# Two sparse attention layers on one Trainium2 core: where the selection of a block's keys ranks among the attention's steps

## The chip, the cores and the metric

The kernel runs on one core of one Trainium2 chip. The metric is the device time in microseconds (us) of one execution; the smaller the better. TensorE (PE in the profile) multiplies matrices into PSUM; VectorE (DVE), ScalarE (ACT) and GpSimd (POOL) do the elementwise work; SyncE (SP) starts the weights' transfers. Each engine works off its own instructions in the order in which the built program has them, and waits where an instruction's inputs or buffers are not ready.

## The reference

The model takes 512 tokens of width 1024 through one block of a first kind and then two layers of a second kind. The change lies in the second kind's sparse attention, cut here to what matters:

```python
def dsa_attention(q, k, v, qi, ki, wi):        # T = 512, 8 heads of 64; topk = 128; blocks of 128 queries
    def block_fn(args):
        rel = jax.nn.relu(jnp.einsum('bqhd,bsd->bqhs', qib, ki32))      # 4 index heads
        score = jnp.einsum('bqh,bqhs->bqs', wib, rel)
        score = jnp.where(visible[None], score, -jnp.inf)               # key_pos <= qpos
        _, idx = lax.top_k(score, topk)
        k_sel, v_sel = gather(k, idx), gather(v, idx)
        logits = jnp.einsum('bqhd,bqkhd->bhqk', qb, k_sel) * scale      # masked by idx <= qpos
        p = jax.nn.softmax(logits, axis=-1)
        return jnp.einsum('bhqk,bqkhd->bqhd', p, v_sel)
```

Beside this attention each layer runs a gated recurrence of four heads (hgrn) on the same input. Both results go through a projection, are weighted by sigmoid gates and added, and a feed-forward part follows. Queries and keys are normed by head and rotated (RoPE) before the attention.

## The kernel before

All weights are streamed from HBM in 512 KB pieces; ScalarE and GpSimd or VectorE split each piece into a high and a low part (`whi`, `wlo`, lines 149 and 152), and each product is three matmuls (lines 168 to 170 where the output has tokens on the partitions, 193 to 195 where it has features). One such matmul of 512 columns is called wide here; a projection of one 128 wide column tile is 24 of them.

A layer of the second kind (`second_mix`) first writes down the attention (`dsa`), then the four recurrence heads, each with three projections (hf, hq, hg) and a chain of small steps (lines 466 to 515), then two merges: the attention's with eight gate projections and eight output projections (`gate`, `merge`), then the recurrence's. A scheduler orders the instructions of each engine: what is written earlier ranks ahead of what is written later, weights and evictions ahead of all, and what is not ready by its reckoning lets later work pass. So the recurrence heads' projections and the first three gate projections fill the attention's waits on TensorE.

Within the attention the string `ORDER` (line 25) says in which order the steps are written down:

- `x`: the projection of the index inputs; `h`: that of the recurrence's values; `X`: rotation and transposes of the index inputs (line 863), from which come `iqT` and `ikT`.
- `1`, `2`, `3`: `select(i)`, the selection of block i's keys. For each of four index heads TensorE multiplies (line 874) into w = (i+1)*128 columns, ScalarE takes the Relu (876) and VectorE weights and adds (879, 881); after a mask (882) come 16 rounds in which `max` finds the eight largest scores of each row (885) and `match_replace` marks them as taken (886); line 887 turns the marks into a bias. Block 0 needs no selection, since it has 128 keys.
- `k`, `q`, `v`: the projections of keys, queries and values; ScalarE copies them out and squares them (810, 812), VectorE sums the squares (813). `K`: rotation of the keys (`rotated`): the square root's steps (229 to 233), two products on VectorE and two on GpSimd for each block (799 to 802), the scaling (825), and the transposes on TensorE (239).
- `Q`: the same for one block of queries at each call; its results `qT` are kept until the attention of that block.
- `a` to `d`: `attend(i)`, the attention of blocks 0 to 3. For each of eight heads: scores on TensorE (925), bias and negative maximum on VectorE (927), the exponential on ScalarE (929), transposes (933), a copy (935), and the products with the values (937) into one PSUM tile. Then the division (939, 941), transposes (239) and the split into high and low (217, 218).

All PSUM tiles of the attention's lane are drawn from two banks (`BANKS`, tag `pa`). During `attend` the output tile holds one, so that a head's scores and its transposes take turns in the other.

The loop that writes the steps down, and the rounds of the selection:

```python
        for c in ORDER:
            if c in steps:
                steps[c]()
            elif c in "123":
                select(int(c))
            else:
                attend("abcd".index(c))

            for r in range(16):
                m8 = self.small("m8", 8)
                nc.vector.max(m8, sc[:, 0:w])
                nc.vector.match_replace(sc[:, 0:w], m8, sc[:, 0:w], TAKEN)
```

Of the kernel before, what the change touches and what calls it, by code (L numbers as in the profile page):

```python
# [21 lines left out]
KD = 8  # L22
KF = 22
WARM = 12
ORDER = "xhX123kKqvQaQbQcQd"
EPS = 1e-6
NEG = -1e30
UNSEEN = -2e38
# [42 lines left out]
class Builder:  # L71
# [756 lines left out]
    def dsa(self, l, X):  # L828
# [61 lines left out]
        def inputs(j, name):  # L890
            got[name] = self.attention_inputs(A["w_tok"][l, j], X, name)
# [23 lines left out]
        def attend(i):  # L915
# [27 lines left out]
            for m in range(4):  # L943
# [3 lines left out]
                     q=lambda: inputs(1, "aq"), Q=rotate_query, v=values, h=gated_values)  # L947
        for c in ORDER:
            if c in steps:
# [155 lines left out]
```

## Time and profile before

| what | value |
|---|---|
| median of three runs | 2590.12 us (2587.59 to 2593.46) |
| the profiled execution's own time | 2592.11 us |
| its span, first to last instruction | 2590.3 us |
| mean granted clock of TensorE | 0.99 |
| attention and recurrence, first layer of the second kind | from about 876 to 1310 us of the span |
| the same, second layer | from about 1730 to 2168 us |

The span is the time from the first to the last instruction; the execution's own time has 1.8 us around it. In the sections below, "first layer" and "second layer" are these two. A matmul's busy time in the trace is longer than the spacing of two matmuls that follow each other, since they overlap; the spacing is the price of one in a full stretch. The granted clock is 1.00 at 2.4 GHz and 0.50 at 1.2 GHz.

### The profile page before, as it was taken

Reading aid. Unit: us, or ns where it says so; the run is one execution under the profiler, and the core shown is the slowest. Engines: PE = TensorE matmul, PEld = TensorE weight load, DVE = VectorE, ACT = ScalarE, POOL = GpSimd, SP = SyncE. Lnnn points to the kernel's source line nnn. Section 1 sums busy time; section 2 is a strip of 40 time slices with the busy share of each in tenths; the row PEclk is TensorE's granted clock in tenths of the full one; section 3 lists DMA queues with packets and bytes.
Section 4 is the critical chain, followed back from the end, with each engine's and each line's share of the span. In section 5 each row is a group of like instructions: output and inputs, shape, how many; then the busy total and the mean of one; then the engine's idle time right before and its main releaser. Section 6 shows DMA issues by size and latency. Waiting matters only on the chain.

```text
span 2590.3 us, 31616 instructions
## 1 busy us (share of the span) xinstructions
PE 2504.4 (97%) x11742; PEld 2047.2 (79%) x11742; DVE 1362.4 (53%) x2568; ACT 1011.7 (39%) x1830; POOL 769.8 (30%) x676
## 2 busy tenths in 40 slices
PE   9999999999999998899999999999798999999999
PEld 7877888888888766777888888887677788888887
DVE  4675222477764677765244444336877523444432
ACT  5633333444443344453343333334355333433322
POOL 4234334511101333643361110013465335211100
PEclk9999999999999999999999999999899999999999
DMA  4112233322233222111332223332211123222233
GB/s 136 58 60 82 87 97 98 102 98 98 97 95 96 76 74 73 42 37 59 94 99 98 97 94 95 94 98 66 73 42 40 34 96 101 96 94 96 97 108 88
DMA packets 67434, 217.66 MB, mean 84 GB/s; under 512 B 7744, under 2 KB 8640, under 8 KB 67280
## 3 DMA queue, kind: packets, MB, share of 16 engines
q1 hardware_dynamic: 67280, 215.65, 26.1%
q8 instruction: 92, 1.51, 0.2%
q14 instruction: 62, 0.51, 0.1%
HBM read 213.52 MB, written 2.10 MB: 83 GB/s over the span
## 4 chain that ended last, share of the span: by engine, by line
PE 80%; DVE 14%; POOL 3%; issue 2%; ACT 1%; DMA 0%; SPq 0%; DVEq 0%; POOLq 0%; ACTq 0%
PE mm L194 23%; PE mm L195 23%; PE mm L193 23%; DVE score L886 2%; DVE m L885 2%; PE at L925 1%; PE at L937 1%; PE at L239 1%; DVE wlo L152 1%; POOL hG L495 1%; PE mm L169 1%; PE mm L170 1%; PE mm L168 1%; DVE rsq_w L231 1%; PE at L933 1%
## 5 line engine op out<-in xcount | busy, mean ns | idle before, releaser
L149 ACT CAST whi<-wraw 128x512 fp32r<-128x512 f32 (+3 forms) x824 | 502.3, 610 | 1139.9 <-PE mm L195 950.4
L193 PE MATMUL mm<-xh,wlo 128*128 128x512 f32 x1920 | 759.0, 395 | 0.0
L194 PE MATMUL mm<-xl,whi 128*128 128x512 f32 x1920 | 758.2, 395 | 0.0
L195 PE MATMUL mm<-xh,whi 128*128 128x512 f32 x1920 | 755.5, 393 | 0.0
L152 DVE TENSOR_TENSOR wlo<-wraw,whi 128x512 fp32r<-128x512 f32 (+1 forms) x529 | 385.2, 728 | 458.5 <-ACT whi L149 455.4
L152 POOL TENSOR_TENSOR wlo<-wraw,whi 128x512 fp32r<-128x512 f32 (+2 forms) x295 | 381.4, 1293 | 760.5 <-ACT whi L149 689.6
L195 PEld LDWEIGHTS mm<-xh,whi 128*128 128x128 f32 x1920 | 361.8, 188 | 74.5 <-issue 1.9
L194 PEld LDWEIGHTS mm<-xl,whi 128*128 128x128 f32 x1920 | 361.9, 188 | 73.5 <-issue 1.7
L193 PEld LDWEIGHTS mm<-xh,wlo 128*128 128x128 f32 x1920 | 361.8, 188 | 72.9 <-issue 1.2
L193 PE MATMUL mm<-acth,wlo 128*128 128x512 f32 x528 | 205.4, 389 | 0.0
L194 PE MATMUL mm<-actl,whi 128*128 128x512 f32 x528 | 205.4, 389 | 0.0
L195 PE MATMUL mm<-acth,whi 128*128 128x512 f32 x528 | 205.4, 389 | 0.0
L733 POOL TENSOR_TENSOR fg<-fg,rstd 128x512 f32<-128x512 f32 x44 | 56.7, 1289 | 425.6 <-ACT fg L732 425.6
L168 PE MATMUL mm<-wlo,xh 128*128 128x512 f32 (+2 forms) x384 | 147.0, 383 | 17.3 <-POOL wlo L152 9.2
L169 PE MATMUL mm<-whi,xl 128*128 128x512 f32 (+2 forms) x384 | 145.2, 378 | 0.2 <-DVE xl L288 0.2
L170 PE MATMUL mm<-whi,xh 128*128 128x512 f32 (+2 forms) x384 | 145.1, 379 | 0.0
L202 DVE TENSOR_TENSOR gate<-mm,rstd 128x512 f32<-128x512 f32 x56 | 38.7, 691 | 165.2 <-PE mm L195 164.3
L277 POOL TENSOR_TENSOR acc<-acc,sq 128x512 f32<-128x512 f32 x39 | 58.9, 1509 | 199.2 <-ACT sq L274 198.3
L194 PEld LDWEIGHTS mm<-actl,whi 128*128 128x128 f32 x528 | 99.1, 188 | 20.8
L193 PEld LDWEIGHTS mm<-acth,wlo 128*128 128x128 f32 x528 | 99.1, 188 | 20.6
L195 PEld LDWEIGHTS mm<-acth,whi 128*128 128x128 f32 x528 | 99.1, 188 | 20.4
L168 PEld LDWEIGHTS mm<-wlo,xh 128*128 128x128 f32 x384 | 73.4, 191 | 36.1 <-POOL wlo L152 11.7
(352 smaller groups left out, 3333.1 us busy)
## 6 DMA issues: line engine op xcount, KB each, us to landing
wraw<-in_w_ffn_in SPq DMA_DIRECT2D x88, 512.0 KB, 3.3
wraw<-in_w_gate SPq DMA_DIRECT2D x56, 512.0 KB, 3.3
wraw<-in_w_in SPq DMA_DIRECT2D x52, 512.0 KB, 3.3
wraw<-in_w_up SPq DMA_DIRECT2D x44, 512.0 KB, 3.2
wraw<-in_w_tok SPq DMA_DIRECT2D x32, 512.0 KB, 3.2
wraw<-in_w_ffn_out SPq DMA_DIRECT2D x32, 512.0 KB, 3.6
wraw<-in_w_down SPq DMA_DIRECT2D x16, 512.0 KB, 3.6
wraw<-in_w_po SPq DMA_DIRECT2D x32, 256.0 KB, 2.6
```

The lines of the kernel that those rows point to most:

```text
L149: nc.scalar.copy(wh, raw[:, k:k + m, :])
L152: eng.tensor_tensor(wl, raw[:, k:k + m, :], wh.bitcast(F32), op=OP.subtract)
L168: nc.tensor.matmul(ps[t][:, 0:w], xh, wl, start=i == 0, stop=False)
L169: nc.tensor.matmul(ps[t][:, 0:w], xl, wh, start=False, stop=False)
L170: nc.tensor.matmul(ps[t][:, 0:w], xh, wh, start=False, stop=i == KD - 1)
L193: nc.tensor.matmul(ps, wl, xh, start=i == 0, stop=False)
L194: nc.tensor.matmul(ps, wh, xl, start=False, stop=False)
L195: nc.tensor.matmul(ps, wh, xh, start=False, stop=i == n - 1)
L277: (nc.vector if d % 2 and len(acc) > 1 else nc.gpsimd).tensor_tensor(a, a, sq, op=OP.add)
L733: nc.gpsimd.tensor_tensor(g, g, self.rstd, op=OP.mult)
L885: nc.vector.max(m8, sc[:, 0:w])
L886: nc.vector.match_replace(sc[:, 0:w], m8, sc[:, 0:w], TAKEN)
```

## The change

One string is changed. The selections no longer stand together ahead of the keys' projection: each stands just ahead of its block's attention. And two blocks of queries are rotated ahead of the first attention, and each later block one attention earlier.

```diff
-ORDER = "xhX123kKqvQaQbQcQd"
+ORDER = "xhXkKqvQQa1Qb2Qc3d"
```

What this does to the engines' orders is shown at three places of the first layer; the second layer's change in the same way. (A row is one instruction or several equal ones; `score` is the selection's row of scores, `m` the eight largest, `ak` and `rsq` belong to the keys' norm, `rope` and `aro` to rotation, `aon` to the division at an attention's end, `csts` holds the identity for transposes.)

**VectorE, where the keys are normed and rotated.** Before, between the rounds of the second selection:

```order
L813 TENSOR_REDUCE akss<-asq 128x8 x2
L885 MAX m_7689<-score 128x8
L820 TENSOR_SCALAR akss<-akss 128x32
L800 TENSOR_TENSOR rope_7968<-akx,tabS 128x8x32
L152 TENSOR_TENSOR wlo<-wraw,whi 128x512
L886 MATCH_REPLACE score<-m_7689,score 128x384
L229 TENSOR_SCALAR rsq_y<-akss 128x32
L801 TENSOR_TENSOR rope_7968<-akx,tabS 128x8x32
L885 MAX m_7692<-score 128x8
L231 TENSOR_TENSOR rsq_w<-akss,rsq_y 128x32
```

Now:

```order
L800 TENSOR_TENSOR rope_7755<-akx,tabS 128x8x32
L813 TENSOR_REDUCE akss<-asq 128x8 x2
L801 TENSOR_TENSOR rope_7755<-akx,tabS 128x8x32
L820 TENSOR_SCALAR akss<-akss 128x32
L229 TENSOR_SCALAR rsq_y<-akss 128x32
L231 TENSOR_TENSOR rsq_w<-akss,rsq_y 128x32
L152 TENSOR_TENSOR wlo<-wraw,whi 128x512
L232 SCALAR_TENSOR_TENSOR rsq_w<-rsq_w,rsq_y 128x32
```

The selection's rounds have gone from this place; the keys' steps follow each other with only the weights' split between them.

**TensorE, at the last block's attention (512 keys).** Before, the step from one of its heads to the next:

```order
L193 MATMUL mm<-xh,wlo 128x512
L933 MATMUL at<-csts,aL 128x128 x4
L194 MATMUL mm<-xl,whi 128x512
L195 MATMUL mm<-xh,whi 128x512
L193 MATMUL mm<-xh,wlo 128x512
L194 MATMUL mm<-xl,whi 128x512
L937 MATMUL at<-av,aPT 128x64 x4
L925 MATMUL at<-kT,qT 128x512
```

Now, from the end of the third block's attention (384 keys) into the last's:

```order
L925 MATMUL at<-kT,qT 128x384
L933 MATMUL at<-csts,aL 128x128 x3
L937 MATMUL at<-av,aPT 128x64 x3
L239 MATMUL at<-csts,aon 128x128 x4
L874 MATMUL at<-ikT,iqT 128x512 x4
L925 MATMUL at<-kT,qT 128x512
L933 MATMUL at<-csts,aL 128x128 x4
L937 MATMUL at<-av,aPT 128x64 x4
```

The wide matmuls of gate projections that stood between the steps of a head now stand ahead of the third block's attention, and the third selection's score matmuls (874) stand between the two attentions.

**VectorE, at the same place.** Before, two heads of the last block, with steps of the fourth recurrence head around them:

```order
L514 TENSOR_TENSOR hf<-hf,hq 128x512
L927 ISA aL,anm<-at,score 128x512
L927 ISA anm 128x1
L399 COPY rS<-at 128x128
L401 SCALAR_TENSOR_TENSOR rS<-rS,dec,at 128x128 x2
L411 TENSOR_REDUCE rss<-rsq 128x4
L412 TENSOR_SCALAR rss<-rss 128x4
L229 TENSOR_SCALAR rsq_y<-rss 128x4
```

Now, between the third block's last head and the last block's first:

```order
L939 RECIPROCAL aden<-aden 128x8
L941 TENSOR_TENSOR aon<-at,aden 128x512
L218 TENSOR_TENSOR yal<-at,yah 128x128 x2
L879 TENSOR_SCALAR score<-rel,iw 128x512
L218 TENSOR_TENSOR yal<-at,yah 128x128
L212 TENSOR_TENSOR yhl<-ry,yhh 128x512 x2
```

Behind these rows come the rest of the third selection's scores and its 16 rounds, and only then the last block's eight heads; the fourth recurrence head's steps now lie ahead of all this.

## Rows read from the trace of the kernel before

**Rows 1.** The page's first part: TensorE's busy time, share of the span.

```profile
PE 2504.4 (97%) x11742; PEld 2047.2 (79%) x11742; DVE 1362.4 (53%) x2568; ACT 1011.7 (39%) x1830; POOL 769.8 (30%) x676
```

**Rows 2.** Busy time by stretch; four of the first layer, one of the second.

```profile
core 0: us, PE busy (x) PEld busy (x) DVE busy (x) ACT busy (x) POOL busy (x), PEclk, DMA share, GB/s
924.00:1017.00 93.00, 81.18 (x334) 61.42 (x335) 86.48 (x207) 37.96 (x80) 34.37 (x28) 0.94 0.21 68
1017.00:1049.00 32.00, 28.90 (x157) 22.63 (x157) 19.88 (x46) 18.77 (x41) 14.62 (x17) 1.00 0.16 51
1049.00:1198.00 149.00, 136.61 (x832) 108.89 (x832) 109.81 (x253) 70.05 (x143) 74.78 (x82) 1.00 0.11 35
1198.00:1310.00 112.00, 112.00 (x500) 92.84 (x500) 33.13 (x52) 36.73 (x63) 38.92 (x30) 1.00 0.30 92
...
1901.00:2057.00 156.00, 144.25 (x834) 115.61 (x834) 110.69 (x257) 69.94 (x143) 79.27 (x85) 0.95 0.10 33
```

**Rows 3.** TensorE's waits, 876 to 1310: us, times, longest.

```profile
PE at L239 <- DVE aro L825: 13.6, 4, 8.3
...
PE at L933 <- ACT aL L929: 2.2, 1, 2.2
```

**Rows 4.** VectorE's groups by shape, 924 to 1021: busy us, mean ns, idle before.

```profile
L885 DVE MAX8 m<-score 128x8 f32<-128x512 f32 x16 | 11.1, 691 | 0.2
L886 DVE MATCH_REPLACE8 score<-m,score 128x512 f32<-128x512 f32 x16 | 10.8, 675 | 0.0
L885 DVE MAX8 m<-score 128x8 f32<-128x384 f32 x16 | 8.8, 553 | 0.2
L886 DVE MATCH_REPLACE8 score<-m,score 128x384 f32<-128x384 f32 x16 | 8.6, 540 | 0.0
L885 DVE MAX8 m<-score 128x8 f32<-128x256 f32 x16 | 6.8, 425 | 0.3
L886 DVE MATCH_REPLACE8 score<-m,score 128x256 f32<-128x256 f32 x16 | 6.5, 408 | 0.0
...
L881 DVE SCALAR_TENSOR_TENSOR score<-rel,iw,score 128x512 f32<-128x512 f32 x3 | 3.1, 1048 | 0.0
```

**Rows 5.** VectorE in order of time: start, us; the third selection's rounds undisturbed.

```profile
1012.65 0.69 DVE L885 MAX8 m<-score 128x8 f32<-128x512 f32 x1
...
1018.73 0.69 DVE L885 MAX8 m<-score 128x8 f32<-128x512 f32 x1
```

**Rows 6.** In order of time: a head of block d, first layer, full clock.

```profile
1189.40 0.69 DVE L927 CUSTOM_DVE_ANT_0 aL<-at,score 128x512 f32<-128x512 f32 x1 [0.29 <-PE at L925]
...
1191.06 0.66 PE L933 MATMUL at<-csts,aL 128*128 128x128 f32 x4
...
1191.81 0.59 ACT L935 COPY aPT<-at 128x512 f32<-128x512 f32 x1 [0.18 <-PE at L933]
...
1192.48 1.07 PE L937 MATMUL at<-av,aPT 128*128 128x64 f32 x8
1193.39 1.08 PE L925 MATMUL at<-kT,qT 128*128 128x512 f32 x2
...
1194.51 0.69 DVE L927 CUSTOM_DVE_ANT_0 aL<-at,score 128x512 f32<-128x512 f32 x1 [0.56 <-PE at L925]
```

**Rows 7.** In order of time: block d's heads, second layer, half clock.

```profile
2031.17 1.92 PE L937 MATMUL at<-av,aPT 128*128 128x64 f32 x8
...
2032.88 2.02 PE L925 MATMUL at<-kT,qT 128*128 128x512 f32 x2
...
2034.94 0.69 DVE L927 CUSTOM_DVE_ANT_0 aL<-at,score 128x512 f32<-128x512 f32 x1 [1.58 <-PE at L925]
...
2038.97 1.06 PE L933 MATMUL at<-csts,aL 128*128 128x128 f32 x4
...
2040.12 0.59 ACT L935 COPY aPT<-at 128x512 f32<-128x512 f32 x1 [1.09 <-PE at L933]
```

**Rows 8.** Busy time and granted clock in that stretch.

```profile
2031.00:2041.00 10.00, 10.00 (x42) 8.11 (x42) 4.95 (x12) 2.31 (x5) 4.75 (x5) 0.50 0.00 0
```

## The prediction

> **What bounds the kernel now.** I read the page's first part, then the stretches of the first attention layer, then who TensorE waited for in it, then the DVE rows of the selection, and last one head of attention in order of time. TensorE is busy 97% of the span [rows 1], so a change can win only TensorE's idle and slow time, and loses as soon as another engine takes over the pace. In the stretches [rows 2] this idle time is nearly all in the two attention layers: of 93 us from the last index transpose to the first score matmul of block a, TensorE is busy for 81 at a granted clock of 0.94; of the 149 us from block a's normalisation (L941) to block d's it is busy for 137; the 112 us behind are full, and their 500 matmuls give one wide (512 column) matmul per 0.224 us.
>
> In the first of these stretches DVE is the pacing engine: 86 of 93 us busy [rows 2]. It runs the three selections, and the rotation of the keys stands between their rounds. TensorE therefore waits for rotated keys: 13.6 us in four waits, one of 8.3, and 2.2 us more for block a's first softmax, which stands behind the third selection [rows 3]. In the 149 us stretch DVE is busy for 110, so 39 us are free. These 39 us and the wait for the keys are what the change plays with.
>
> **What the change moves.** No instruction is added or removed; the order of the engines shows what goes where.
>
> First stretch (93 us). The index matmuls (12 instructions) and the three selections leave it, and the second block's query rotation comes in behind the value projection, hidden there. TensorE then has 286 wide matmuls (counted in the order) x 0.224 = 64 us, and 24 transposes at some 0.11 = 3 us. A wait for the keys stays: between the last key matmul and the first transpose stand only 38 wide matmuls, 8.5 us, while the norm and two rotations need ScalarE's four pairs of evictions (about 5 us behind the last matmul, an estimate) and some 10 us of DVE. That is a wait of about 6.5 us, between nothing and the present 10; the slow clock behind such a wait costs about 4 more, as now (the 0.94 of [rows 2]). Sum 78, **15 us less** per layer (11 to 26).
>
> Block a (32 us). Its order stays; the 2.2 us wait behind the third selection [rows 3] goes. **2 us less.**
>
> From a's L941 to d's L941 (149 us). Each selection is 16 rounds of MAX and MATCH_REPLACE. By their means [rows 4] the rounds are 16 x (0.69 + 0.68 + 0.55 + 0.54 + 0.43 + 0.41) = 53 us. Rounds that follow each other directly take 1.52 us each at 512 keys (four in 6.08 us [rows 5]), 0.15 above the two means, so 60 us with nothing in between. Nine multiply-adds at 1.05 or less [rows 4] and a few small instructions add 4 to 9. I take 64 us of new DVE work, between 57 and 69. One query rotation (about 2.6 us) goes out. So DVE has 110 + 64 - 3 = 171 us to do in what was 149. That alone is 22 us over, and it can't be packed, because of the tail:
>
> - In the order of TensorE, the last wide matmul (of the third gate projection) now stands ahead of the transposes of block c's first head. Behind it come c's heads with only the small matmuls of the fourth recurrence head between them, then the third selection's four score matmuls, then d's heads with nothing between them at all. Wide matmuls filled these waits before.
> - A head is a serial chain: scores, reduction, exponent, transposes, copy, value matmul, next scores. At full clock it takes 5.11 us from one L927 to the next with 512 keys [rows 6]. Where the clock was 0.50 [rows 8], value matmuls to scores took 1.71 instead of 0.91, scores to L927 2.06 instead of 1.12, transposes to copy 1.15 instead of 0.75 [rows 6, 7]: 5.11 + 0.80 + 0.94 + 0.40 = 7.25 us.
>
> Piece by piece: (1) Up to the end of the second selection DVE sets the pace. Of its 171 us, c's stretch holds about 17, the third selection 30, d 6; 118 remain, and I add 8 for waits: 126 (118 to 160, the last if DVE keeps waiting as it does now, 110 busy in 149). Here the new waits stand at the first transposes of blocks b and c: they want a softmax that wants the selection, and the recurrence heads' and gates' projections queued behind them on TensorE wait too; what hides them otherwise, some 265 wide matmuls or 59 us, is less than DVE's 118. The twelve Relu of the scores on ScalarE and GpSimd's two products of the moved rotation lie beside this DVE work and cost nothing while it lasts. (2) Block c: eight heads at 384 keys, by estimate 4.4 us each at full clock (between three quarters and all of 5.11) or 6 at half, with some DVE work of the last recurrence head ahead of the second: 36 to 48, I take 41. (3) c's normalisation and transposes 3, scoring 5, 16 x 1.52 = 24 and the marking: 33 us in which TensorE has nothing but four score matmuls. (4) Block d: seven pitches and a last head of about 6: 57 at half clock, 41.5 at full. In the trace the clock fell to 0.5 behind long idle, and during the ten us at 2031 [rows 8] TensorE was busy throughout with small matmuls and still did not get it back, so I take half clock. Sum 126 + 41 + 33 + 57 = 257: **108 us more** than 149. At full clock 126 + 36 + 33 + 41.5 = 236.5: 87.5 more.
>
> Behind d. 33 wide matmuls that stood behind d's end are now done ahead of it: 7.5 us less, but the next projection needs d's split result at once, which takes 3 us to fill and a slow start of 1 us: **3.5 us less**. The weights' transfers are no bound: the same sequence of loads, at 35 GB/s there and 92 in the full stretch [rows 2].
>
> Sum, first layer: 108 - 15 - 2 - 3.5 = +87. The second layer's order changes in the same way, and its stretch was 156 us already [rows 2], 7 more: +80. Together +167 us on the profiled execution's own 2592.1 us: 2759, and with the median 2 us below that execution **2757 us**.
>
> **The rivals.**
>
> Full clock (rival 1): TensorE's small matmuls suffice to hold its clock in the tail. 87.5 - 20.5 = +67, second layer +60: 2592 + 127 - 2 = 2717 us. For it: in the first layer block d ran at full clock throughout; against it: wide matmuls stood between then, and the second layer fell to half all the same [rows 7, 8].
>
> Waits pile up (rival 2): the recurrence heads' steps go from DVE to GpSimd to TensorE and back, and each in-order queue may hold up the others, so that DVE idles as large a share as today. Piece (1) is then 160 instead of 126, 34 more per layer: 2757 + 68 = 2825 us. For it, 39 idle us in 149 today; against it, selection rounds are ready work that stands between those steps, and where they do so today DVE is busy 86 of 93 us.
>
> The selection hides (rival 3, not slower): all three selections run in DVE's idle 39 us while TensorE goes on with wide matmuls, and the keys come early. Only the gains stay, 17 us a layer: 2590 - 34 = 2556 us. It decides at 39 us of DVE time and at wide matmuls left to cover the third selection; 57 us are needed at the least [rows 4, 5], and no wide matmul is left there. The Trainium skill's page "Perfetto Trace Analysis", section "Optimization Strategy", says that where the most-contended engine changes over time, interleaving these regimes may help, and that is what this order does with DVE's and TensorE's. By that rule it would be this rival's 2556; the rows speak against it, since both stretches together hold fewer free DVE us than the tail exposes.
>
> The order hardly matters (rival 4): the time stays within 0.2%, about what a measurement of this kernel can tell from no change. It would need losses and gains to cancel within 5 us.
>
> **How the numbers follow.** Forecast 0.50, rival 1 0.25, rival 2 0.19, rival 3 0.04, rival 4 0.02. The range 2695 to 2825 holds the forecast with the spread of its terms, rival 1 and the lower half of rival 2, a bit over 0.8. Faster 0.04, same 0.02, slower 0.94.
>
> **What would show it.** Right: the last key transposes and block a's scores come some 15 us earlier; from a's L941 to d's some 255 us instead of 149 and 156; no wide matmul from c's first transposes to behind d, and a gap of some 30 us of TensorE ahead of d, with only the third selection on DVE; d's L927 7.25 us apart at half clock, 5.1 at full. Wrong: wide matmuls between d's heads in the trace, heads in the tail that overlap each other, or DVE more than a fifth idle between a's end and the second selection's (rival 2).

## The result, and the profile after

The changed kernel takes 2775.57 us (median of four runs, 2771.93 to 2784.64) against 2588.86 for the kernel before (2587.22 to 2593.46): a ratio of 1.0723, with a 95% interval of 1.0693 to 1.0754. It is slower by 187 us. The forecast was 2757, with a range of 2695 to 2825.

The page's first part and the granted clock by fortieths of the span (the kernel after; to set beside [rows 1]):

```profile
span 2770.0 us, 31579 instructions
...
PE 2571.1 (93%) x11742; PEld 2081.4 (75%) x11742; DVE 1369.8 (49%) x2568; ACT 1002.9 (36%) x1822; POOL 773.0 (28%) x676
...
PEclk9999999999999999955999999999998579999999
```

TensorE runs the same 11742 matmuls and is busy longer for them (2571 us instead of 2504), and still its share fell from 97% to 93%: it both waits more and runs slower. The clock line says where: two short stretches near 5, one at the end of each sparse attention, where the line of before shows none.

The stretches of the first layer (the kernel after; busy time by engine, then the granted clock; to set beside [rows 2]). The cuts are block a's first scores, a's L941, the second selection's end (L887), c's L941, the third selection's end, and d's L941:

```profile
core 0: us, PE busy (x) PEld busy (x) DVE busy (x) ACT busy (x) POOL busy (x), PEclk, DMA share, GB/s
922.00:1002.00 80.00, 72.46 (x316) 57.84 (x314) 38.31 (x56) 32.86 (x70) 40.25 (x32) 0.96 0.24 79
1002.00:1032.00 30.00, 28.80 (x158) 22.77 (x157) 16.06 (x38) 19.62 (x43) 14.81 (x17) 1.00 0.17 55
1032.00:1156.00 124.00, 111.60 (x623) 89.77 (x624) 113.19 (x287) 44.19 (x89) 67.38 (x74) 0.99 0.14 47
1156.00:1203.00 47.00, 34.66 (x145) 24.88 (x143) 16.87 (x49) 12.98 (x29) 5.35 (x6) 0.60 0.02 6
1203.00:1240.00 37.00, 9.53 (x16) 3.53 (x15) 30.38 (x63) 5.30 (x12) 0.00 (x0) 0.55 0.00 0
1240.00:1297.00 57.00, 36.89 (x109) 22.68 (x110) 6.22 (x18) 11.19 (x24) 0.00 (x0) 0.50 0.01 3
```

VectorE's 86 of 93 us ahead of block a have become 38 of 80, and the first stretch is 13 us shorter. What left it comes back behind: from a's L941 to d's it now takes 265.6 us instead of 149.6. In the first 124 of these VectorE is busy for 113; in the 37 us of the third selection it is busy for 30, and TensorE runs 16 matmuls; in block d neither is full, and the clock is 0.50.

TensorE's longest waits in the same layer (us in total, times, longest; to set beside [rows 3]):

```profile
PE at L933 <- ACT aL L929: 46.3, 14, 27.5
PE at L937 <- ACT aPT L935: 9.7, 14, 0.7
PE at L239 <- DVE aro L825: 9.4, 5, 5.7
...
PE at L874 <- ACT rel L876: 1.7, 3, 0.7
```

The wait for rotated keys and queries has fallen from 13.6 to 9.4. (Only 8.3 of the 13.6 was the keys', in one wait; the other three waits, 5.3 us, lie behind block a and were for rotated queries.) Instead TensorE waits 46.3 us for softmaxes, 27.5 of it in one piece: the third selection, on the way to block d's first transposes. The fourteen waits for the copied transposes are those of bare heads, with no other matmul between the steps. Waits of the selection's score matmuls (874) for a Relu to read out their PSUM tile come to 1.7 us in all, so sharing two banks with the attention costs them little.

The end of that selection, in order of time (start, us; in brackets the idle time ahead and what ended it):

```profile
1213.72 1.02 PE L925 MATMUL at<-kT,qT 128*128 128x512 f32 x2
...
1240.00 0.43 DVE L887 TENSOR_SCALAR score<-score 128x512 f32<-128x512 f32 x1
1240.57 0.69 DVE L927 CUSTOM_DVE_ANT_0 aL<-at,score 128x512 f32<-128x512 f32 x1
...
1242.23 1.12 PE L933 MATMUL at<-csts,aL 128*128 128x128 f32 x4 [27.48 <-ACT aL L929]
...
1244.08 1.97 PE L937 MATMUL at<-av,aPT 128*128 128x64 f32 x8 [0.73 <-ACT aPT L935]
1245.84 2.02 PE L925 MATMUL at<-kT,qT 128*128 128x512 f32 x2
1247.90 0.69 DVE L927 CUSTOM_DVE_ANT_0 aL<-at,score 128x512 f32<-128x512 f32 x1 [6.63 <-PE at L925]
```

The scores of d's first head were done at 1214.7. Then TensorE stands still for 27 us. From one L927 to the next there are 7.3 us, as in the half-clock pieces of [rows 7].

### The profile page after: what moved, and what is told of

The parts are those of the page before. It is cut to its first block, busy times and chain, and to the rows that moved or that the text cites. A ratio compares the mean times of both kernels' runs of the same rounds, so it can differ in the third digit from the quotient of the medians.

```text
span 2770.0 us, 31579 instructions
## 1 busy us (share of the span) xinstructions
PE 2571.1 (93%) x11742; PEld 2081.4 (75%) x11742; DVE 1369.8 (49%) x2568; ACT 1002.9 (36%) x1822; POOL 773.0 (28%) x676
## 4 chain that ended last, share of the span: by engine, by line
PE 79%; DVE 13%; ACT 3%; issue 2%; POOL 2%; DMA 0%; SPq 0%; ACTq 0%; DVEq 0%; POOLq 0%
PE mm L195 21%; PE mm L194 21%; PE mm L193 21%; PE at L937 2%; PE at L925 2%; PE mm L168 2%; PE mm L169 2%; PE mm L170 2%; DVE score L886 1%; DVE m L885 1%; PE at L933 1%; PE at L239 1%; ACT aL L929 1%; DVE aL L927 1%; PE at L509 1%
## 5 line engine op out<-in xcount | busy, mean ns | idle before, releaser
L933 PE MATMUL at<-csts,aL 128*128 128x128 f32 x160 | 40.5, 369 | 91.2 <-ACT aL L929 91.0
L933 PEld LDWEIGHTS at<-csts,aL 128*128 128x128 f32 x160 | 24.9, 186 | 126.8 <-ACT aL L929 125.1
```

What stands on the lines that cost most here:

```text
L933: nc.tensor.transpose(pt[:, kb, :], L[:, kb * P:(kb + 1) * P], self.ident)
```

## The experiments

Each kernel below ran on the chip beside the kernel before, whose median was 2588 to 2589 us in every set. All but e5, e9 and e10 change only the string `ORDER`. My theory was that the selections do the harm, in two ways: VectorE is given more than it can carry up to the second selection's end, and behind that end block c, the third selection and block d stand in a row with no wide matmul beside them. The first rival was that the queries' lookahead does it; the second, that it is mainly the clock.

### Which half of the change: e1, e2

```diff
-ORDER = "xhX123kKqvQaQbQcQd"
+ORDER = "xhX123kKqvQQaQbQcd"    (e1: the queries ahead alone)
+ORDER = "xhXkKqvQaQ1bQ2cQ3d"    (e2: the selections late alone)
```

> Only the second half of the change: the queries are rotated one block ahead, the three selections stay together ahead of the keys. My theory (the loss comes from the selections: VectorE sets the pace up to the second selection's end, and behind it stands a tail without wide matmuls) expects about the time before, 2580 to 2600 us, with block d's heads still among wide matmuls. The rival that the lookahead of the queries is to blame (two GpSimd products and four rows of steps moved in front of the first attention) expects a good part of the 186 us here, 2640 us or more.

> Only the first half: each selection ranks just ahead of its block's attention, the queries' rotation stays behind it as before. My theory expects the whole loss, 2776 us within 15, with the stretch from block a's L941 to block d's at 255 to 275 us in the first layer and some 35 us of bare third selection in it. The rival that the lookahead is to blame expects the time before, about 2590.

e1: 2585.92 us, ratio 0.9984 (0.9974 to 0.9993). e2: 2803.58 us, ratio 1.0823 (1.0802 to 1.0845). The rival with the lookahead falls: alone it gains 3 us, and the selections alone make the whole loss. My figure for e2 missed by 28 us, and its stretch from a's L941 to d's takes 279.1 us, above the 255 to 275 expected: without the lookahead the loss is larger than that of the full change. In e2's trace a→b, b→c and c→d (L941 to L941, first layer) take 87.0, 95.9 and 96.2 us, where the changed kernel has 79.9, 91.6 and 94.1. Each block's query rotation there stands behind the attention ahead of it, in front of that block's selection, on the VectorE that sets the pace. So the lookahead takes some 28 us off the harm of the late selections; that the rotation's place on VectorE is how it does so is argued from the order, not tried apart.

Where e1's 3 us come from, block d of the second layer shows, in the one profiled execution of each (e1, 50 us from c's L941 to d's; then the kernel before, 60 us):

```profile
2000.00:2050.00 50.00, 47.92 (x282) 36.88 (x282) 34.33 (x85) 22.42 (x45) 21.98 (x23) 1.00 0.09 27
```

```profile
1997.00:2057.00 60.00, 56.06 (x300) 44.54 (x299) 40.65 (x91) 25.59 (x49) 23.17 (x25) 0.89 0.07 23
```

Before, block d of the second layer ran partly at the half clock of [rows 8]; in e1 it does not. In the first layer, which had a clock of 1.00 there already, the same piece is 4 us shorter too (49.4 instead of 53.1), so some 6 of the 10 us are the clock's, an estimate; but the first layer as a whole gained nothing (447.0 us from the last L863 to the next norm's L254, 444.9 before).

### What each part of the loss costs: e3, e4

```diff
-ORDER = "xhX123kKqvQaQbQcQd"
+ORDER = "xhX12kKqvQQaQbQc3d"    (e3: only the third selection late)
+ORDER = "xhX3kKqvQQa1Qb2Qcd"    (e4: the third early, the first two late)
```

> As the changed kernel, but the first and second selection go back to their old place ahead of the keys; only the third stands late. My theory prices the parts of the loss: VectorE has no more than it can carry up to block c, c's heads keep their wide matmuls (some 28 us instead of 48), the third selection stands bare except for what is left of the wides, and d's heads are bare and at half clock (57 us instead of 28 among wides). That makes some 44 us a layer over before, about 2676 us (2650 to 2710). A theory in which the third selection alone makes the loss (its 37 us of gap and all behind it) expects 2740 or more; one in which VectorE's load makes all of it expects under 2620.

> The other way round: the third selection goes back ahead of the keys, the first and second stay late. My theory: the 37 us gap ahead of block d goes, the first stretch grows by the part of the third selection's 30 us that hides nothing (15 to 25 us), and c's and d's heads still have few wide matmuls, so about 2730 us (2690 to 2760). If the bare third selection were the whole loss, this would come back to 2590 to 2610.

e3: 2670.89 us (ratio 1.0311, 1.0291 to 1.0332; expected 2676). e4: 2723.25 us (1.0513, 1.0492 to 1.0534; expected 2730). Neither part makes the loss alone: some 82 us with the third selection late, some 134 with the first two, 187 with all. That the two sum to more than the whole fits what they share: block d's bare heads stand in both. Their stretches (e3: c's L941 to the third selection's end, then block d; e4: a's L941 to the second selection's end, then blocks c and d):

```profile
1138.00:1188.00 50.00, 41.85 (x204) 32.22 (x203) 49.23 (x109) 16.90 (x30) 21.24 (x24) 0.95 0.15 48
1188.00:1245.00 57.00, 39.11 (x135) 25.57 (x135) 12.34 (x39) 14.17 (x28) 0.00 (x0) 0.56 0.01 3
```

```profile
1040.00:1164.00 124.00, 108.83 (x611) 87.49 (x611) 115.09 (x286) 46.29 (x94) 66.27 (x72) 1.00 0.14 47
1164.00:1214.00 50.00, 37.65 (x154) 28.20 (x154) 17.79 (x55) 12.91 (x29) 6.58 (x8) 0.58 0.03 6
1214.00:1275.00 61.00, 40.20 (x116) 24.22 (x116) 7.73 (x23) 12.13 (x28) 0.00 (x0) 0.50 0.01 3
```

In e3 the third selection has wide matmuls beside it (TensorE busy for 42 of 50 us). Those are then missing in block d, which takes the same 57 us as in the changed kernel; from c's L941 to d's it is 107 us, 53 before. In e4 the 124 us with VectorE at 115 are there again, with two selections in them.

### Whether VectorE sets the pace there: e10

```diff
-            for r in range(16):
+            for r in range(8):
```

> The changed kernel with 8 rounds of selection instead of 16 in each block (64 keys are then chosen, half of the computation's selection is left out). By the rows of before the third selection's gap loses 8 x 1.52 = 12 us, and the first two selections lose 8 x (0.43 + 0.41 + 0.55 + 0.54) = 15 us of VectorE's work. If VectorE sets the pace up to the second selection's end, as I hold, all of it comes off: 27 us a layer and a few more from wide matmuls that are left for block c, 2700 to 2725 us. If that stretch is held up by waits from engine to engine rather than by VectorE's work, only the gap shrinks: about 2750 us.

2684.94 us, ratio 1.0371 (1.0352 to 1.039): 91 us off the changed kernel, more than either theory gave. The same stretches as above (a's L941, second selection's end, c's L941, third selection's end, d's L941):

```profile
1033.00:1130.00 97.00, 86.13 (x472) 69.03 (x473) 82.35 (x198) 42.30 (x82) 50.43 (x57) 0.96 0.13 44
1130.00:1171.00 41.00, 37.98 (x254) 31.26 (x253) 31.14 (x74) 15.73 (x35) 20.19 (x22) 1.00 0.08 27
1171.00:1196.00 25.00, 13.74 (x57) 8.80 (x56) 23.60 (x56) 8.61 (x18) 2.55 (x2) 0.84 0.10 32
1196.00:1253.00 57.00, 37.07 (x110) 22.85 (x110) 6.17 (x18) 11.19 (x24) 0.00 (x0) 0.50 0.01 3
```

The third selection is 12 us shorter, as its rounds say. The first piece went from 124 to 97, and VectorE's busy time in it from 113 to 82: the piece follows VectorE's work. 15 us of that are the rounds; the rest are steps of the last recurrence head, which now lie in block c (VectorE 31 there, 17 in the changed kernel), and block c carries them at no price: with wide matmuls left beside it (79 of them start behind the second selection's end, 4 in the changed kernel), at a clock of 1.00, it takes 41 us instead of 47. Block d, bare as ever, takes the same 57. The rival, that the first piece is held up by waits from engine to engine, falls. What I had missed is that saved VectorE time is worth more than itself here, because it also leaves wide matmuls for the block behind.

### The clock: e5, e9

e5 gives TensorE something to do in each round of the third selection; e9 does that too and adds a matmul to each of block d's heads, where TensorE waits for the softmax (the first added line is in both, the second in e9 alone):

```diff
                 nc.vector.max(m8, sc[:, 0:w])
+                i == 3 and nc.tensor.matmul(ps[0:8, :], m8, got["kT"][0], start=True, stop=True)
...
                 for kb in range(i + 1):
+                    kb == 0 and i == 3 and nc.tensor.matmul(pt.rearrange("p n c -> p (n c)"), self.ident, kT[0], start=True, stop=True)
                     nc.tensor.transpose(pt[:, kb, :], L[:, kb * P:(kb + 1) * P], self.ident)
```

> The changed kernel with one matmul added to each of the third selection's 16 rounds (the round's eight largest scores times a key tile, 512 columns in float32, the result unused): TensorE now has some 1.1 us of work at full clock, 2 at half, in each round of 1.5 us, where it had nothing. Nothing else moves. It separates the clock from the waits. If the empty 37 us hold the clock down and small matmuls then can't bring it back, the clock now stays or returns to 1.00 there, and block d's heads come 5.1 us apart instead of 7.3: 15 us a layer less, about 2745 us. If block d's own matmuls can't keep the clock whatever stood ahead, it stays at 0.50 and the time stays within 10 us of the changed kernel's 2776. If the clock is not what makes d's heads slow, they come 7.3 us apart at a clock of 1.00.

> The kernel of the run before with a matmul in each round of the third selection, and one more in each head of block d: between a head's scores and its transposes, while TensorE waits for the softmax, it multiplies the identity by a key tile (512 columns, float32) into the transposes' tile, which the transposes then overwrite; added work, its result unused. The chain of a head has nothing more to wait for at full clock (1.1 us of matmul against some 2 us of softmax). If it is TensorE's small share of work in a bare head that costs it the clock, the clock now stays at 1.00 through block d, its heads come some 5.1 to 5.5 us apart instead of 7.3, and the time falls by some 14 to 17 us a layer, to about 2745. If the clock falls all the same, the heads come 7.3 us apart or more, and the time is 2772 or more.

e5: 2773.99 us, ratio 1.0725 (1.0706 to 1.0743): no different from the changed kernel. e9: 2740.88 us, ratio 1.0584 (1.0561 to 1.0607): 35 us less. First e5: the start of the third selection, its scoring, its 16 rounds with the added matmuls, and block d from within its first head. Then e9: the third selection and block d of the first layer, and block d of the second:

```profile
1200.50:1204.30 3.80, 2.82 (x6) 1.25 (x6) 1.27 (x3) 0.63 (x3) 0.00 (x0) 0.50 0.00 0
1204.40:1211.50 7.10, 4.06 (x8) 1.27 (x8) 6.46 (x13) 4.47 (x10) 0.00 (x0) 1.00 0.00 0
1211.50:1236.20 24.70, 16.39 (x32) 1.56 (x32) 22.74 (x48) 0.00 (x0) 0.00 (x0) 1.00 0.00 0
...
1238.50:1292.90 54.40, 36.52 (x108) 22.25 (x106) 5.10 (x15) 10.38 (x22) 0.00 (x0) 0.50 0.01 3
```

```profile
1200.60:1238.00 37.40, 25.24 (x46) 4.91 (x46) 30.33 (x62) 5.30 (x12) 0.00 (x0) 0.87 0.00 0
1238.00:1278.90 40.90, 28.25 (x127) 15.33 (x126) 6.28 (x20) 11.20 (x24) 0.00 (x0) 1.00 0.01 4
...
2172.30:2215.60 43.30, 30.74 (x127) 16.37 (x126) 6.21 (x18) 11.19 (x24) 0.00 (x0) 0.92 0.00 0
```

In e5 the clock is back at 1.00 during the scoring, at 1204.4, ahead of the first added matmul (1211.6). In the changed kernel it comes back there too, at 1213.4, and is gone at 1216.8; the added matmuls hold it through the selection. Block d then loses it within its first head: the heads come 7.3 us apart at 0.50, as if nothing had been done. In e9 the clock stays at 1.00 through block d of the first layer, which takes 41 us instead of 57. In the second layer it falls in the first two heads, for 7 us, and comes back among the heads themselves (43 us instead of 57). One head of the first layer in order of time:

```profile
1248.71 0.69 DVE L927 CUSTOM_DVE_ANT_0 aL<-at,score 128x512 f32<-128x512 f32 x1 [4.40 <-PE at L925]
...
1249.46 1.12 PE L933 MATMUL at<-kT,csts 128*128 128x512 f32 x2 [0.79 <-DVE anm L927]
...
1250.42 0.60 PE L933 MATMUL at<-csts,aL 128*128 128x128 f32 x4
...
1251.76 1.10 PE L937 MATMUL at<-av,aPT 128*128 128x64 f32 x8 [0.73 <-ACT aPT L935]
...
1252.70 1.08 PE L925 MATMUL at<-kT,qT 128*128 128x512 f32 x2
1253.81 0.69 DVE L927 CUSTOM_DVE_ANT_0 aL<-at,score 128x512 f32<-128x512 f32 x1 [4.41 <-PE at L925]
```

With one matmul more in it a head is faster: 5.1 us from L927 to L927, the value of [rows 6], where the bare head takes 7.3. So the slow clock in block d is not left over from the idle time ahead; the bare head itself brings it about, and costs some 15 us a layer by it. (The matmul in the heads alone, without those in the selection, was not tried.) That is 35 of 187 us. These runs leave the slow heads of block c as they are; by the prediction's price for them at full clock (36 us, where the changed kernel takes 47.6 and 44.6) they would add some 20 us in both layers, an estimate. The rival that it is mainly the clock falls.

### Versions that were to keep the gain: e6, e7, e8, e11

```diff
-ORDER = "xhX123kKqvQaQbQcQd"
+ORDER = "xhXkK12qvQa3QbQcQd"    (e6)
+ORDER = "xhXkK1q2vQa3QbQcQd"    (e7)
+ORDER = "xhXkK123qvQaQbQcQd"    (e8)
+ORDER = "xhX1kK23qvQQaQbQcd"    (e11)
```

> A version meant to take the change's gain without its loss: the keys are projected and rotated ahead of all selections, the first two selections stand between them and the queries, the third behind block a's attention, the queries' rotation where it was before. By the order all selections then have wide matmuls beside them, and every block's heads keep theirs up to the end of block d. My theory expects the keys' wait to go and nothing to come back: 2550 to 2575 us. The rival that any selection among the attention's steps costs what it takes on VectorE (30 us of it for the third) expects 2600 or more.

> As the version with the keys first, but the queries' projection stands between the first and the second selection. My theory: the same within 10 us, 2550 to 2575.

> Only the keys' projection and rotation go ahead of the selections, which stay together. My theory: the wait for rotated keys goes, but block a's first softmaxes wait longer for the three selections' end on VectorE, some 5 to 15 us: 2565 to 2590 us.

> The queries one block ahead as in the change, all three selections ahead of the attention as before, but the keys' projection and rotation between the first and the second. By the order every head keeps its wide matmuls as before, and 39 of them stay behind block d's end for its split. My theory: no loss, and the wait for rotated keys (13.6 us in the kernel before) loses 3 to 8 us a layer: 2570 to 2582 us. If that wait is only pushed elsewhere, the time is that of the kernel with the queries ahead alone, 2586.

e6: 2594.96 us, ratio 1.0024 (1.0014 to 1.0034). e7: 2594.92 us, 1.0025 (1.0013 to 1.0037). e8: 2603.82 us, 1.0059 (1.0044 to 1.0075). e11: 2582.78 us, 0.9979 (0.9969 to 0.999). The first three lie 14 to 20 us above the upper end of what I expected, and on the wrong side of the kernel before. The large losses are gone, as the order said: every head has wide matmuls beside it, but for one or two at the end of block d. But no gain is left either. e6's first layer as a whole, its longest waits of TensorE, and the same stretch of the kernel before:

```profile
922.00:1372.00 450.00, 422.21 (x2069) 336.08 (x2068) 278.03 (x590) 187.99 (x366) 200.26 (x181) 0.98 0.20 66
...
PE at L239 <- DVE aro L825: 9.3, 5, 5.7
PE at L933 <- ACT aL L929: 5.7, 5, 2.8
```

```profile
924.00:1369.00 445.00, 416.52 (x2072) 332.89 (x2072) 276.58 (x590) 189.16 (x367) 196.55 (x181) 0.99 0.21 67
```

TensorE is idle for 27.8 of 450 us in e6 and 28.5 of 445 before. The wait for rotation fell by 4 us, the wait for softmaxes rose by 3.5, and the clock is a little lower. Of the 13.6 us that seemed to be there for the taking, nothing is left in the end. The pieces show where it goes. e6 reaches block a's first scores 7 us earlier (85.5 us instead of 92.7) and gives that back behind: block a takes 34.2 instead of 32.2, and from a's L941 to d's it takes 164.1 instead of 149.6, with VectorE busy for 138 instead of 110 (e6, then before):

```profile
1041.50:1205.60 164.10, 151.10 (x877) 117.61 (x877) 137.94 (x311) 74.76 (x152) 79.18 (x84) 0.99 0.11 38
```

```profile
1049.10:1198.70 149.60, 137.31 (x837) 109.59 (x838) 110.34 (x254) 70.07 (x143) 74.68 (x82) 1.00 0.11 35
```

In this longer piece e6 uses up all its wide matmuls. The last one starts at 1199.1, and no other stands beside block d's last head and the split of its output; the clock is at 0.50 from 1205.3 to 1212.2. In the kernel before 32 are left over for that place. Behind d's L941 e6 is only 3.4 us shorter for it (167.0 instead of 170.4). In e8 block a pays, as its expectation said (39.9 and 47.1 us in the two layers instead of 32.2 and 33.6), but the stretch ahead of it gains only 3 to 4 us.

e11 leaves the selections ahead of the attention and beats the kernel before by 6 us; it came out just above what I expected, its interval overlaps that of e1, and its gain lies where e1's does: the second layer takes 445.9 us instead of 452.7 (last L863 to L254), the first 447.2 instead of 444.9. That moving the keys' rotation itself gains something is not shown.

## Why the prediction was right

The sign, the size and the way were as forecast; 2757 was 19 us short. In the profiled executions the change costs 179.8 us (2592.11 and 2771.93), 13 more than the sum's 167; the other 6 us lie between these executions and the medians. By its steps, first layer:

- **First stretch**: forecast 78 us, measured 79.4 (from 922.7 to 1002.1), with a rest of the wait for rotation (longest 5.7 us, forecast 6.5). The gain was real, though the prediction read all 13.6 us of the wait as the keys': theirs was 8.3. Block a: forecast 30, measured 29.8.
- **Piece 1**, up to the second selection's end: forecast 126, measured 123.9, VectorE busy for 113 (forecast 118). That VectorE's work sets it was shown by e10, and by e4 with the same two selections. Rival 2, waits that pile up, would have shown VectorE idle for a quarter; it was idle for a tenth.
- **Block c** is the term most off: forecast 41, measured 47.6. I had its heads between full and half clock. By the trace the first took 8.8 us, with the recurrence's steps ahead on VectorE, the next two 5.5 and 4.3, and the other four 5.9 to 6.0, at the half clock (0.60 over the stretch). Of the prediction's two ends the upper one, 48, was nearer here. The block varies: it took 44.6 in the second layer, and 43.2 and 43.5 in the first layers of e5 and e9, whose instructions are the same up to its end.
- **The third selection**: forecast 33, measured 36.6. The 16 rounds took the 24.3 us of [rows 5]; the normalisation, transposes and scoring ahead of them took 12.3 instead of 8, at the half clock (a score matmul takes 1.9 to 2.1 us there, and waits for a Relu to free its bank) and with splits of the recurrence's output between the steps on VectorE.
- **Block d**: forecast 57 at half clock, measured 57.5, 7.3 us a head. The price was right, and its reason only in part. I argued from idle time ahead and from small matmuls that did not bring the clock back; e5 shows that the idle time doesn't decide it, since a clock that is full at block d's start is lost in it. The ten us of [rows 8] show less than I read in them: five wide matmuls stand among the small ones, and behind these the clock came back, at 2041.2. Rival 1 needed the small matmuls to hold the clock, and they did not; in e9, where each head has one matmul more, it held or came back, block d took 17 and 14 us less in the two layers, and the kernel 35.
- **Behind d**: forecast 3.5 us less, measured 4.3 less (L941 of d to L254: 166.1 us, 170.4 before).

The sum for the first layer was +87 and is +96, 540.9 us from the last L863 to L254 instead of 444.9; the second +80 and is +85. Block c and the third selection's scoring, 10 us in the first layer, are the difference, less the 2 us by which piece 1 was shorter. Rival 3, in which the selection hides, fails by 219 us (2775.57 against 2556): the interleaving did shorten VectorE's own stretch, by 13 us, but the wide matmuls that TensorE was to run beside the selections were used up before the third one began (the last starts at 1156.8, the third selection's first score matmul at 1205.0). Rival 3 is what the Trainium skill's page "Perfetto Trace Analysis", section "Optimization Strategy", points to, where it says that interleaving regimes with different most-contended engines may help; the trace does not bear that out here.

## What to carry to other kernels

Before an engine's heavy stretch is spread into another's, count what that other has left to run beside it, to the end: here 640 wide matmuls a layer (counted in the order, up to the attention's output projection) had covered the chains, and once they are gone each further step costs its full length. A wait that the profile shows (13.6 us here) is not a gain of that length: e6 to e8 shortened it to 9 or 10 us, and the work that they moved out of its way cost as much or more behind it. Keep some independent work for the end of the chain too: e6 ran out of it one head early. And a serial chain without filler can lose TensorE's clock by itself, so that added work which nobody uses may make it faster (e9, by 35 us).

## What the runs showed of the hardware that was not expected

In block d the clock went by what the block's own heads gave TensorE to do, not by what stood ahead of them. In the changed kernel it stays at 0.50 for 85 us: through the last 23 us of the third selection, in which TensorE has nothing to do, and the whole of block d, though TensorE has work in every head (the kernel after, both layers):

```profile
1217.00:1302.00 85.00, 40.75 (x119) 25.50 (x120) 30.81 (x72) 12.25 (x28) 0.00 (x0) 0.50 0.01 2
2163.00:2247.00 84.00, 43.05 (x125) 27.27 (x126) 26.89 (x62) 12.26 (x28) 0.00 (x0) 0.50 0.00 0
```

In e5 the clock was at 1.00 from 1204.4 on, through the added matmuls, and fell to 0.50 at 1238.5, in the first of the bare heads that followed. In e9, with an added matmul in each head, it stayed at 1.00 in the first layer; in the second it fell at 2176.5 and was back at 2183.3, while the same kind of head went on. At 0.50 a bare head's scores take 2.02 us instead of 1.08 and its value matmuls 1.97 instead of 1.10; with the waits between them a head grows from 5.1 to 7.3 us.
